# A row of token scales for two feed-forwards: matmuls with ones against a trip through DRAM

## The chip, the cores and the metric

One core of a Trainium2 chip runs one launch of the kernel. The metric is the device time of that launch in microseconds (us), the median of several runs.

## What is computed

The layer works on 256 tokens of 1024 channels, in fp32. It has a feed-forward, a mixer of three branches (retention, differential attention, attention into 256 memory tokens) and a second feed-forward. Only the feed-forwards matter here:

```
x = x + 0.5 * (silu(h @ wg) * (h @ wu)) @ wd      with  h = rms_norm(x) * gain
```

with `wg` and `wu` of 1024 x 2816 and `wd` of 2816 x 1024. The norm is one number r per token, 1/sqrt(mean(x^2) + eps). Since r is constant along the channels, the kernel multiplies `x * gain` by the weights first and applies r to the product.

## The kernel before, in words

**Products in three parts.** Every weight tile is split into a rounded part `hi` (ScalarE, L131) and a rest `lo` (VectorE, L134, in two halves); activations are split in the same way. A product is the sum of three matmuls. The results of gate and up lie with hidden channels on partitions and the 256 tokens along the free axis, so r is needed there as a row of 256 numbers that is the same on all 128 partitions.

**The feed-forward (`ffn`, L296).** The hidden width is cut into 11 blocks of 256. `gate_up(j)` multiplies block j of gate and up (weights loaded on SyncE's queue at L123; matmuls at L167 with `hi`, at L172 with `lo`) and joins the parts on ScalarE (L182) and VectorE (L183) into a tile `jo`. `hidden` turns the two `jo` of a block into the operand of the down product: L303 multiplies gate's tile by the row `rb` on VectorE, L304 takes Silu on ScalarE, L305 multiplies by up's tile on VectorE, L308 (ScalarE) and L309 (VectorE) split the product into `ah` and `al`. The down matmuls (L191, L192, L194) accumulate into `acc`. Blocks 0 and 1 of gate and up run ahead of the row, and then block 2 runs on TensorE before the down product of block 0.

**The row (`token_rstd`, L483, and `rows_to_free`, L234).** ScalarE sums the squares of x (L488), VectorE makes the mean (L231), GpSimd raises it to -0.5 (L226): r, two numbers on each of 128 partitions. L238 multiplies the identity by r's two columns, two diagonal tiles `dg`; L239 multiplies a matrix of ones by them in fp32 on TensorE, which spreads the row to all partitions in a PSUM bank; L241 copies it to `rb`. L492 makes r/2 for the residual.

**What sets the order.** A planner sorts the instructions of each engine by its own estimate of when their operands are ready, and by the order in which the program names them; each engine then runs its list strictly in that order. `keep(...)` pins an instruction behind the one that the program named last on the same engine. `tc.issue_after(i)` puts what its block names on the engine of i behind i: block 2's VectorE work stands behind `st["dg"]` (L323), which is the second diagonal tile. Tiles of `mid` (`jo`, `dg`, `rb`, `ah`, `al` among them) share 14 slots, and the two PSUM tags `pj` and `at` have four banks each.

**GpSimd's queue around the change.** GpSimd runs r (L226) and then, pinned behind it, the load of the columns of gains `vcol` (L363, called by the hook of block 1). These gains are first used by ScalarE at L245 on the memory tokens.

The lines that the steps touch most:

```python
def rows_to_free(r, alloc):
    dg = mid([NT, P], F32, "dg")
    ps = alloc([S])
    for t in range(NT):
        st["dg"] = V.tensor_scalar_mul(dg[:, t, :], ident, r[:, t:t + 1]).ins
        keep(T.matmul(ps[:, t * P:(t + 1) * P], ones, dg[:, t, :], start=True, stop=True))
    rb = mid([S], F32, "rb")
    V.tensor_copy(rb, ps)
    return rb
```

Of the kernel before, what the change touches and what calls it, by code (L numbers as in the profile page):

```python
# [11 lines left out]
F32 = mybir.dt.float32  # L12
# [7 lines left out]
P = 128  # L20
D = 1024
S = 256
NT = S // P
# [33 lines left out]
def layer_kernel(ctx, tc, a):  # L57
    nc = tc.nc
    V, A, G, T = nc.vector, nc.scalar, nc.gpsimd, nc.tensor
    keep = tc.keep_in_program_order  # L60
# [3 lines left out]
    wp = ctx.enter_context(tc.tile_pool(name="wp", bufs=3))  # L64
    tp = ctx.enter_context(tc.tile_pool(name="tp", bufs=14))
    sp = ctx.enter_context(tc.tile_pool(name="sp", bufs=24))
    pp = ctx.enter_context(tc.tile_pool(name="pp", bufs=4, space=PSUM))

    cnt = [0]

    def nm(s):
        cnt[0] += 1
        return f"{s}_{cnt[0]}"

    def big(shape, dt=F32, n="g"):
        return gp.tile([P] + shape, dt, tag="g", name=nm(n))

    def mid(shape, dt=F32, n="t"):
        return tp.tile([P] + shape, dt, tag="t", name=nm(n))

    def small(n, nme="s"):
        return sp.tile([P, n], F32, tag="s", name=nm(nme))

    def const(shape, n, dt=F32):
        return cp.tile([P] + shape, dt, tag=n, name=n)

    def psj(shape):
        return pp.tile([P] + shape, F32, tag="pj", name=nm("pj"))

    def psa(shape):  # L90
        return pp.tile([P] + shape, F32, tag="at", name=nm("at"))
# [22 lines left out]
    def wchunk(w, k0, kt, n0, n, deint=False, parts=1):  # L114
        shape = [kt, n]
        raw = wp.tile([P] + shape, F32, tag="raw", name=nm("raw"))
        hi = wp.tile([P] + shape, F32R, tag="hi", name=nm("hi"))
        lo = wp.tile([P] + shape, F32R, tag="lo", name=nm("lo"))
        src = w[k0 * P:(k0 + kt) * P, n0:n0 + n].rearrange("(k p) n -> p k n", p=P)
        step = kt // parts  # L120
        for q in range(parts):
            c = slice(q * step, (q + 1) * step)
            nc.sync.dma_start(raw[:, c, :], src[:, c, :])  # L123
        for q in range(parts):
            c = slice(q * step, (q + 1) * step)
            rv, hv, lv = raw[:, c, :], hi[:, c, :], lo[:, c, :]
            hb = hv.bitcast(F32)
            if deint:
                rv = rv.rearrange("p k (i e) -> p k e i", e=2)
                hv, lv, hb = (v.rearrange("p k (e i) -> p k e i", e=2) for v in (hv, lv, hb))  # L130
            A.copy(hv, rv)  # L131
            h = step // 2
            for e in (slice(0, h), slice(h, step)):
                V.tensor_sub(lv[:, e], rv[:, e], hb[:, e])  # L134
        return hi, lo
# [50 lines left out]
    def mm_b(ps, w, xT, t, k0, kt, first, last, c0=0, n=512):  # L186
        hi, lo = w
        tk = slice(t * P, (t + 1) * P)
        c = slice(c0, c0 + n)
        for k in range(kt):  # L190
            T.matmul(ps, xT.h(k0 + k)[:, tk], hi[:, k, c], start=(first and k == 0), stop=False)  # L191
            T.matmul(ps, xT.l(k0 + k)[:, tk], hi[:, k, c], start=False, stop=False)  # L192
        for k in range(kt):
            T.matmul(ps, xT.h(k0 + k)[:, tk], lo[:, k, c], start=False, stop=(last and k == kt - 1))  # L194
# [19 lines left out]
    def proj_s(w, n0, xT, deint=False, alloc=None):  # L214
        ps = [(alloc or psj)([2, S]) for _ in range(2)]
        wc = wchunk(w, 0, KT, n0, 256, deint)
        mm_s(ps, wc, xT, turns=alloc is not None)
        return joined(ps)


    st = {}
# [9 lines left out]
        V.tensor_scalar(ms, ss, 1.0 / count, EPS, ALU.mult, ALU.add)  # L231
        return pow_rstd(ms, n, out)

    def rows_to_free(r, alloc):  # L234
        dg = mid([NT, P], F32, "dg")
        ps = alloc([S])
        for t in range(NT):
            st["dg"] = V.tensor_scalar_mul(dg[:, t, :], ident, r[:, t:t + 1]).ins  # L238
            keep(T.matmul(ps[:, t * P:(t + 1) * P], ones, dg[:, t, :], start=True, stop=True))  # L239
        rb = mid([S], F32, "rb")  # L240
        V.tensor_copy(rb, ps)  # L241
        return rb

    def split_gain(src, col, hi, lo):
# [5 lines left out]
    vcol = const([NCOL], "vcol")  # L250
# [3 lines left out]
    def col(i):  # L254
        return vcol[:, i:i + 1]

    ident = const([P], "ident")
    ones = const([P], "ones")
# [37 lines left out]
    def ffn(xT, w, rb, hooks, first, alloc, end=None):  # L296
        wg, wu, wd = w
        acc = []
        state = {}

        def hidden(sg, av):
            rv = state["rb"].unsqueeze(1).broadcast_to([P, 2, S])
            V.tensor_mul(sg, sg, rv)  # L303
            A.activation(sg, sg, AF.Silu)  # L304
            V.tensor_mul(av, av, sg)  # L305
            ah = mid([2, S], F32R, "ah")
            al = mid([2, S], F32R, "al")
            A.copy(ah, av)  # L308
            V.tensor_sub(al, av, ah.bitcast(F32))  # L309
            return Hidden(ah, al)  # L310

        def gate_up(j, alloc=None):
            return proj_s(wg, j * 256, xT, alloc=alloc), proj_s(wu, j * 256, xT, alloc=alloc)

        raw = [first, gate_up(1, alloc)]
        state["rb"] = rb()
        ready = [hidden(*p) for p in raw]
        for j in range(NPAIR):
            aT = ready.pop(0)
            if j in hooks:  # L320
                hooks[j]()
            if j == 0:
                with tc.issue_after(st["dg"]):  # L323
                    ready.append(hidden(*gate_up(j + 2)))
            elif j + 2 < NPAIR:
                ready.append(hidden(*gate_up(j + 2)))
            wc = wchunk(wd, 2 * j, 2, 0, D)
            if j == 0:
                acc = [[psa([512]) for _ in range(2)] for _ in range(NT)]
            if end and j == NPAIR - 2:  # L330
                held = wc, aT
                continue
            if end and j == NPAIR - 1:
                for t, c0, n in end:
                    ps = acc[t][c0 // 512][:, 0:n] if c0 % 512 == 0 else psj([n])
                    fresh = c0 % 512 != 0
                    mm_b(ps, *held, t, 0, 2, fresh, False, c0, n)
                    mm_b(ps, wc, aT, t, 0, 2, False, True, c0, n)
                acc.append(ps)
                continue  # L340
            for t in range(NT):
                for hf in range(2):
                    mm_b(acc[t][hf], wc, aT, t, 0, 2, j == 0, j == NPAIR - 1, hf * 512)
        return acc
# [6 lines left out]
    rows = const([288], "rows")  # L351
# [8 lines left out]
    lamr = rows[:, 32:288].rearrange("p (i d) -> p i d", d=DDK)  # L360

    def vcols():
        keep(G.dma_start(vcol, a["cols"]))  # L363
        keep(V.tensor_scalar_mul(col(G_SUB), col(G_SUB), 1.0 - LAM_INIT))
        keep(V.memset(vcol[0:ROT, G_DQ:G_DQ + 2], 1.0))
        keep(V.memset(vcol[64:64 + ROT, G_DQ:G_DQ + 2], 1.0))
        keep(V.tensor_mul(gqk, vcol[:, G_MQ:G_MQ + 2], vcol[:, G_MK:G_MK + 2]))
# [109 lines left out]
    def stats1():  # L477
        xv = a["x"].rearrange("(t p) d -> p t d", p=P)
        for t in range(NT):
            nc.sync.dma_start(x[:, t, :], xv[:, t, :])  # L480
        return token_rstd(psa, "half1")

    def token_rstd(alloc, name, behind=None):  # L483
        ss = small(NT, "ss")
        j = big([NT, D], F32, "sq")
        with tc.issue_after(behind) if behind else nullcontext():
            for t in range(NT):
                A.activation(j[:, t, :], x[:, t, :], AF.Square, accum_out=ss[:, t:t + 1])  # L488
        r = rstd_of(ss, NT, D)
        rb = rows_to_free(r, alloc)  # L490
        st[name] = const([NT], name)
        V.tensor_scalar_mul(st[name], r, 0.5)  # L492
        return rb

    def mem_load():
# [19 lines left out]
    w1s = (a["ffn1_w_gate"], a["ffn1_w_up"], a["ffn1_w_down"])  # L515
    pgu = first_ffn1()
    acc = ffn(st["xT"], w1s, stats1, hooks, pgu, psj)


# [54 lines left out]
    for b in range(2):  # L574
        ps = proj_b(w_kv, b * 512, memT)
        for t in range(NT):
# [3 lines left out]
            r = rstd_of(ss, 2, MDH)  # L580
# [8 lines left out]
    for b in range(2):  # L589
        ps = proj_b(w_kv, D + b * 512, memT)  # L590
# [58 lines left out]
    for b in range(2):  # L649
        ps = proj_b(w_in, O_MQ + b * 512, hT)  # L650
# [66 lines left out]
    for b in range(2):  # L717
        ps = proj_b(w_in, O_DV + b * 512, hT)
# [213 lines left out]
    for n in range(2):  # L932
        ps = [psj([512]) for _ in range(NT)]
# [9 lines left out]
    acc = [[psa([512]) for _ in range(2)] for _ in range(NT)]  # L943
    xT = Pair("fp")
# [38 lines left out]
    pgu = first_ffn2()  # L983
    gfin = big([D], F32, "gfin")
    G.dma_start(gfin, a["final_norm"].partition_broadcast(P))
    w2s = (a["ffn2_w_gate"], a["ffn2_w_up"], a["ffn2_w_down"])
    end = ((0, 0, 512), (0, 512, 512), (1, 0, 512), (1, 512, 256), (1, 768, 256))
    acc = ffn(xT, w2s, lambda: token_rstd(psj, "half2", st["fp"]), {}, pgu, psa, end)
    ov = a["out"].rearrange("(t p) d -> p t d", p=P)
    o = big([NT, D], F32, "o")  # L990

# [119 lines left out]
```

## Time and profile before

| | before |
|---|---|
| runs, median (lowest to highest of 3) | 878.5 us (878.47 to 878.6) |
| the profiled execution | 878.89 us, of which 877.1 us are the span |
| granted TensorE clock, mean | 0.999 of full speed |
| TensorE matmul busy | 869.6 us, 99% of the span |
| VectorE busy | 603.4 us, 69% |
| ScalarE busy | 444.6 us, 51% |
| GpSimd busy | 41.4 us, 5% |
| moved by DMA | 162.25 MB, 185 GB/s in the mean |

The span is the stretch from the first to the last instruction of the profiled execution; the rest of its time lies around it. PE is TensorE's matmul, PEld its weight load, DVE VectorE, ACT ScalarE, POOL GpSimd, SP SyncE's queue.

### The profile page before, as it was taken

The page shows a single profiled execution, that of the slowest core. Times are in us where ns is not written, and L with a number is a line of the kernel's source. Part 1 is how long each engine was busy: PE and PEld are TensorE (multiplying, and loading weights), DVE is VectorE, ACT ScalarE, POOL GpSimd, SP SyncE. Part 2 cuts the span into 40 slices and gives each one's busy share as a digit, 9 for nine tenths or more (in the row PEclk, how much of TensorE's full clock was granted, in tenths as well). Part 3 has the DMA queues.
Part 4 walks back from the last instruction along what each step waited for, and adds up shares of the span by engine and source line. Part 5 has one row for each costly group of instructions (what it writes and reads, how often), then busy time and mean ns, then how long its engine had stood idle before and what let it go on. Part 6 is the DMA issues. An engine that isn't in the chain of part 4 may idle for free.

```text
span 877.1 us, 11343 instructions
## 1 busy us (share of the span) xinstructions
PE 869.6 (99%) x4436; PEld 738.0 (84%) x4436; DVE 603.4 (69%) x979; ACT 444.6 (51%) x595; POOL 41.4 (5%) x47
## 2 busy tenths in 40 slices
PE   9999999999999999999999999999999999999997
PEld 7888888888888888878888888888888888888885
DVE  6889856667676866669696677665566676666664
ACT  6854644456544445645554444444433665444442
POOL 0010000001032010000100000000000000000000
PEclk9999999999999999999999999999999999999999
DMA  9975555555554554345454555545555466565531
GB/s 340 333 253 192 193 191 190 194 182 175 174 189 166 194 179 159 121 147 174 145 200 151 171 192 192 202 169 190 189 175 197 135 211 218 176 202 189 177 124 49
DMA packets 100693, 162.25 MB, mean 185 GB/s; under 512 B 2896, under 2 KB 55904, under 8 KB 100640
## 3 DMA queue, kind: packets, MB, share of 16 engines
q1 hardware_dynamic: 99648, 159.00, 53.2%
q0 software_dynamic: 848, 2.40, 1.0%
q8 instruction: 35, 0.57, 0.2%
q10 hardware_dynamic: 144, 0.13, 0.0%
q14 instruction: 18, 0.15, 0.0%
HBM read 160.47 MB, written 1.05 MB: 184 GB/s over the span
## 4 chain that ended last, share of the span: by engine, by line
PE 99%; DVE 0%; ACT 0%; POOL 0%; issue 0%; POOLq 0%
PE pj L167 20%; PE pj L191 14%; PE pj L192 14%; PE pj L194 14%; PE pj L172 10%; PE at L192 5%; PE at L191 5%; PE at L194 5%; PE at L261 2%; PE at L201 2%; PE at L460 1%; PE at L167 1%; PE at L735 1%; PE at L463 0%; PE at L276 0%; PE at L172 0%
## 5 line engine op out<-in xcount | busy, mean ns | idle before, releaser
L134 DVE TENSOR_TENSOR lo<-raw,hi 128x1024 fp32r<-128x1024 f32 (+1 forms) x292 | 347.1, 1205 | 173.5 <-ACT hi L131 173.2
L131 ACT CAST hi<-raw 128x2048 fp32r<-128x2048 f32 (+1 forms) x146 | 276.4, 1895 | 259.7 <-issue 132.1
L191 PE MATMUL pj<-hi,hp 128*128 128x512 f32 x352 | 139.3, 396 | 0.0
L192 PE MATMUL pj<-hi,hp 128*128 128x512 f32 x352 | 137.3, 390 | 0.0
L194 PE MATMUL pj<-lo,hp 128*128 128x512 f32 x352 | 94.2, 389 | 0.0
L191 PEld LDWEIGHTS pj<-hi,hp 128*128 128x128 f32 x352 | 66.2, 188 | 13.9 <-issue 1.0
L194 PEld LDWEIGHTS pj<-lo,hp 128*128 128x128 f32 x352 | 66.1, 188 | 13.9
L167 PE MATMUL pj<-fp,hi 128*128 128x512 f32 x320 | 77.5, 391 | 0.0
L192 PEld LDWEIGHTS pj<-hi,hp 128*128 128x128 f32 x352 | 66.2, 188 | 13.0
L167 PE MATMUL pj<-xp,hi 128*128 128x512 f32 x320 | 76.6, 390 | 0.0
L167 PEld LDWEIGHTS pj<-xp,hi 128*128 128x128 f32 x320 | 59.2, 188 | 11.7
L167 PEld LDWEIGHTS pj<-fp,hi 128*128 128x128 f32 x320 | 59.0, 188 | 11.9 <-DVE fp L246 0.4
L192 PE MATMUL at<-hi,al 128*128 128x512 f32 (+1 forms) x176 | 68.2, 388 | 0.0
L191 PE MATMUL at<-hi,ah 128*128 128x512 f32 (+1 forms) x176 | 68.1, 387 | 0.0
L226 POOL TENSOR_TENSOR rstd<-ms,expo 128x2 f32<-128x2 f32 (+3 forms) x26 | 30.0, 1155 | 699.4 <-DVE ms L231 525.5
L194 PE MATMUL at<-lo,ah 128*128 128x512 f32 (+1 forms) x176 | 53.8, 387 | 0.0
L172 PEld LDWEIGHTS pj<-fp,lo 128*128 128x128 f32 x320 | 41.8, 191 | 2.1
L172 PEld LDWEIGHTS pj<-xp,lo 128*128 128x128 f32 x320 | 41.3, 191 | 1.7
L172 PE MATMUL pj<-fp,lo 128*128 128x256 f32 x320 | 42.4, 282 | 0.0
L172 PE MATMUL pj<-xp,lo 128*128 128x256 f32 x320 | 41.8, 283 | 0.0
L194 PEld LDWEIGHTS at<-lo,ah 128*128 128x128 f32 x176 | 32.9, 188 | 6.8
L183 DVE TENSOR_TENSOR jo<-pj,jo 128x256 f32<-128x256 f32 x96 | 36.3, 415 | 3.1 <-ACT jo L182 3.1
(279 smaller groups left out, 1211.2 us busy)
## 6 DMA issues: line engine op xcount, KB each, us to landing
raw<-in_w_in SPq DMA_DIRECT2D x52, 1024.0 KB, 4.8
raw<-in_ffn_w_down SPq DMA_DIRECT2D x22, 1024.0 KB, 4.7
raw<-in_ffn_w_gate SPq DMA_DIRECT2D x20, 1024.0 KB, 5.1
raw<-in_ffn_w_up SPq DMA_DIRECT2D x20, 1024.0 KB, 5.1
raw<-in_mem_w_kv SPq DMA_DIRECT2D x8, 1024.0 KB, 4.9
raw<-in_ret_w_o SPq DMA_DIRECT2D x8, 1024.0 KB, 4.8
raw<-in_mem_w_o SPq DMA_DIRECT2D x4, 1024.0 KB, 4.8
raw<-in_diff_w_o SPq DMA_DIRECT2D x4, 1024.0 KB, 4.7
```

The costliest lines, as they stand in the source:

```text
L131: A.copy(hv, rv)
L134: V.tensor_sub(lv[:, e], rv[:, e], hb[:, e])
L167: T.matmul(ps[nt], hi[:, k, nt * P:(nt + 1) * P], xT.both(k), start=(first and k == k0), stop=False, skip_group_check=True)
L172: T.matmul(ps[nt][:, 0, :], lo[:, k, nt * P:(nt + 1) * P], xT.h(k), start=False, stop=(last and k == k1 - 1), skip_group_check=True)
L183: V.tensor_add(o[:, nt, :], ps[nt][:, 0, :], o[:, nt, :])
L191: T.matmul(ps, xT.h(k0 + k)[:, tk], hi[:, k, c], start=(first and k == 0), stop=False)
L192: T.matmul(ps, xT.l(k0 + k)[:, tk], hi[:, k, c], start=False, stop=False)
L194: T.matmul(ps, xT.h(k0 + k)[:, tk], lo[:, k, c], start=False, stop=(last and k == kt - 1))
L201: T.matmul(o, l, r, start=(i == 0), stop=(i == n - 1))
L226: G.tensor_tensor(r, ms, expo[:, :n], ALU.pow)
L261: T.transpose(out, in_, ident)
L460: T.matmul(ps[nt], hi[:, nt * P:(nt + 1) * P], xT.both(k), start=(k == 0), stop=False, skip_group_check=True)
```

## The change

The diagonal tiles, the fp32 matmuls, the PSUM bank and the copy go. GpSimd's queue stores r (two numbers of each partition) as a row of 256 in a DRAM tile and loads that row back to all 128 partitions. Between the two, the first feed-forward issues the load of `vcol`, which the hook of block 1 no longer issues. `st["dg"]` is now L492's product, so block 2's VectorE work stands behind that.

```diff
+    dp = ctx.enter_context(tc.tile_pool(name="dp", bufs=2, space=bass.MemoryType.DRAM))
...
-    def rows_to_free(r, alloc):
-        dg = mid([NT, P], F32, "dg")
-        ps = alloc([S])
-        for t in range(NT):
-            st["dg"] = V.tensor_scalar_mul(dg[:, t, :], ident, r[:, t:t + 1]).ins
-            keep(T.matmul(ps[:, t * P:(t + 1) * P], ones, dg[:, t, :], start=True, stop=True))
+    def rows_to_free(r, between=None):
+        d = dp.tile([S], F32, tag="rows", name=nm("rows"))
+        keep(G.dma_start(d.rearrange("(t p) -> p t", p=P), r))
+        if between:
+            between()
         rb = mid([S], F32, "rb")
-        V.tensor_copy(rb, ps)
+        keep(G.dma_start(rb, d.partition_broadcast(P)))
         return rb
...
     def vcols():
-        keep(G.dma_start(vcol, a["cols"]))
...
-        return token_rstd(psa, "half1")
-
-    def token_rstd(alloc, name, behind=None):
+        return token_rstd("half1", between=lambda: keep(G.dma_start(vcol, a["cols"])))
+
+    def token_rstd(name, behind=None, between=None):
...
-        rb = rows_to_free(r, alloc)
+        rb = rows_to_free(r, between)
         st[name] = const([NT], name)
-        V.tensor_scalar_mul(st[name], r, 0.5)
+        st["dg"] = V.tensor_scalar_mul(st[name], r, 0.5).ins
...
-    acc = ffn(xT, w2s, lambda: token_rstd(psj, "half2", st["fp"]), {}, pgu, psa, end)
+    acc = ffn(xT, w2s, lambda: token_rstd("half2", st["fp"]), {}, pgu, psa, end)
```

## Rows read from the trace of the kernel before

**Rows 1.** The page: busy time, share of the span and instructions of each engine.

```profile
span 877.1 us, 11343 instructions
PE 869.6 (99%) x4436; PEld 738.0 (84%) x4436; DVE 603.4 (69%) x979; ACT 444.6 (51%) x595; POOL 41.4 (5%) x47
```

**Rows 2.** Waits of PE, whole span: all there are (us in total, times, longest).

```profile
PE at L276 <- DVE expo L273: 1.1, 1, 1.1
```

**Rows 3.** Timeline, first feed-forward, PE (start us, us, engine, line, operation).

```profile
24.96 1.12 PE L172 MATMUL pj<-xp,lo 128*128 128x256 f32 x8
...
25.91 2.00 PE L167 MATMUL pj<-xp,hi 128*128 128x512 f32 x8
...
27.75 1.11 PE L172 MATMUL pj<-xp,lo 128*128 128x256 f32 x8
...
28.70 0.60 PE L239 MATMUL at<-dg,ones 128*128 128x128 f32 x4
...
29.06 3.92 PE L167 MATMUL pj<-xp,hi 128*128 128x512 f32 x16
```

**Rows 4.** Timeline, second feed-forward, PE.

```profile
708.94 1.11 PE L172 MATMUL at<-fp,lo 128*128 128x256 f32 x8
...
709.89 0.60 PE L239 MATMUL pj<-dg,ones 128*128 128x128 f32 x4
...
710.25 3.92 PE L167 MATMUL pj<-fp,hi 128*128 128x512 f32 x16
```

**Rows 5.** Timeline of POOL around the first row.

```profile
23.66 0.72 POOL L226 TENSOR_TENSOR rstd<-ms,expo 128x2 f32<-128x2 f32 x1 [22.35 <-DVE ms L231]
24.33 0.72 POOL L363 DMA_DIRECT2D vcol<-in_cols  x1
43.26 0.54 POOL L403 DMA_DIRECT2D pi<-in_positions  x1 [18.21 <-DVE al L309]
```

**Rows 6.** DMA issues: tile, queue, count, KB each, median us from issue to landing.

```profile
memT<-in_memT SPq DMA_DIRECT2D x1, 1024.0 KB, 9.1
...
out<-o SPq DMA_DIRECT2D x3, 256.0 KB, 2.0
...
rows<-in_rows POOLq DMA_DIRECT2D x1, 144.0 KB, 7.2
pi<-in_positions POOLq DMA_DIRECT2D x1, 128.0 KB, 3.9
...
vcol<-in_cols POOLq DMA_DIRECT2D x1, 15.5 KB, 5.1
...
pci<-in_positions POOLq DMA_DIRECT2D x1, 1.0 KB, 6.9
```

**Rows 7.** Timeline, first feed-forward, DVE from the third `jo` to the first `al`.

```profile
28.78 0.42 DVE L183 TENSOR_TENSOR jo<-pj,jo 128x256 f32<-128x256 f32 x1 [1.91 <-ACT jo L182]
29.12 3.49 DVE L134 TENSOR_TENSOR lo<-raw,hi 128x1024 fp32r<-128x1024 f32 x3
...
32.86 0.41 DVE L241 COPY rb<-at 128x256 f32<-128x256 f32 x1
33.19 1.21 DVE L134 TENSOR_TENSOR lo<-raw,hi 128x1024 fp32r<-128x1024 f32 x1
34.32 1.28 DVE L303 TENSOR_TENSOR jo<-jo,rb 128x512 f32<-128x512 f32 x2
...
39.00 0.68 DVE L309 TENSOR_TENSOR al<-jo,ah 128x512 fp32r<-128x512 f32 x1
```

**Rows 8.** Timeline, first feed-forward: ACT's first use of `vcol`, PE after the row.

```profile
31.80 2.91 ACT L245 ACTIVATE xp<-memT,vcol 128x256 fp32r<-128x256 f32 x7 [0.32 <-DMA memT<-in_memT]
...
32.82 2.08 PE L172 MATMUL pj<-xp,lo 128*128 128x256 f32 x16
...
40.30 0.19 PEld L192 LDWEIGHTS at<-hi,al 128*128 128x128 f32 x1
```

**Rows 9.** Busy us by engine (instructions) in stretches, granted clock, DMA share, GB/s.

```profile
25.00:30.00 5.00, 5.00 (x33) 4.54 (x32) 2.04 (x5) 3.90 (x5) 0.05 (x1) 1.00 1.05 399
30.00:35.00 5.00, 5.00 (x32) 4.42 (x31) 5.00 (x8) 4.39 (x9) 0.00 (x0) 1.00 0.89 319
...
40.00:45.00 5.00, 5.00 (x25) 4.20 (x25) 5.00 (x10) 3.76 (x7) 1.74 (x4) 1.00 0.71 227
```

**Rows 10.** Timeline, second feed-forward: the row's source, DVE's use of it, PE's need.

```profile
697.73 0.17 DVE L492 TENSOR_SCALAR half<-rstd 128x2 f32<-128x2 f32 x1 [0.84 <-POOL rstd L226]
...
713.24 1.28 DVE L303 TENSOR_TENSOR jo<-jo,rb 128x512 f32<-128x512 f32 x2
...
721.49 0.19 PEld L192 LDWEIGHTS at<-hi,al 128*128 128x128 f32 x1
```

## The prediction

> **What bounds the kernel now.** I read the page's first part, then the waits of TensorE, then the timeline around the two places where the row is made. TensorE's matmuls are busy for 869.6 of 877.1 us [rows 1], and the only wait of TensorE that the trace has is 1.1 us at the start [rows 2]. From there to the end TensorE goes from one matmul to the next, so it is the bound in both feed-forwards: what TensorE no longer does comes off the time in full, what the other engines no longer do comes off nothing, and what they do later costs nothing until TensorE waits for it. Two questions are left: how much TensorE time the fp32 matmuls take, and whether the row still comes before its use.
>
> **What is removed from TensorE.** In the first feed-forward the matmuls with ones start at 28.70 and the next product at 29.06 [rows 3]. I take starts, not the busy time of 0.60 us in the same row, since matmuls overlap. The group before them starts at 27.75, which is 0.95 us ahead; an undisturbed change from such a group to the next product is 24.96 to 25.91, also 0.95 us [rows 3]. So the change-over itself costs nothing extra, and the four passes (two matmuls, which the trace shows as x4) hold TensorE for 29.06 - 28.70 = 0.36 us. The second feed-forward has the same: 0.95 from 708.94 to 709.89, then 0.36 to 710.25 [rows 4]. The sum is 2 x 0.36 = 0.72 us. If the busy time were the true cost, it would be 2 x 0.60 = 1.20 us; I keep that as the other end.
>
> **What is removed elsewhere.** VectorE loses two diagonal tiles and one copy of 0.41 us (L241) per feed-forward. VectorE is not the bound [rows 1, 2], so this gains nothing directly; it matters once below, where VectorE's list is tight. The freed PSUM bank and the freed slot of the 14 gain nothing either, as TensorE waits for neither [rows 2].
>
> **What is added: a store and a load, one after the other.** Before, the row's path is r, diagonal, matmul, copy, and ends at 33.27 (32.86 + 0.41) in the first feed-forward [rows 7], though r is there at 24.4 (23.66 + 0.72) [rows 5]: the matmuls are pinned behind block 1's. After, GpSimd issues the store at about 24.4, in the place where it now issues `vcol` (24.33). The load waits for the store to land.
>
> The trace has no store on GpSimd's queue. From below I bound it by the stores of the output on SyncE's queue, 2.0 us; from above by `pci`, a load of the same 256 single numbers in the same arrangement, 6.9 us, which stood behind four other transfers of its queue [rows 6]. I take 5.1 us, that of `vcol`: small, 128 partitions, the same queue, issued at the same moment with the DMA engines just as full (share 1.05 in 25 to 30 us) [rows 6, 9]. For the load the nearest row is `pi`, which is the same shape, 256 numbers spread to 128 partitions, first in its queue: 3.9 us. It ran at a DMA share of 0.71, and mine runs at 0.89 [rows 9], so the upper end is `rows`, 7.2 us; I take 3.9 and keep the upper end [rows 6]. The row then lands at 24.4 + 5.1 + 3.9 = 33.4 us, between 24.4 + 2.0 + 3.9 = 30.3 and 24.4 + 6.9 + 7.2 = 38.5.
>
> [...]
>
> **When the row is needed.** From the start of L303 at 34.32 to the end of the first `al` at 39.68 VectorE has 5.36 us of its list, without a gap [rows 7]. TensorE loads `al` as weights at 40.30 [rows 8]; with 0.36 us gone it asks at 39.94. So L303 may start as late as 39.94 - 5.36 = 34.58 us. The landing at 33.4 leaves 1.2 us. VectorE itself comes to L303 at about 34.0, since the copy (33.19 - 32.86 = 0.33 us of its list) is gone. No wait, at my values; at the upper end 38.5 - 34.58 = 3.9 us of waiting on TensorE.
>
> In the second feed-forward r is there at 697.7, L303 ran at 713.24 and TensorE loads `al` at 721.49 [rows 10]. Even the slow ends, 6.9 + 7.2 us, bring the row at 711.8. This place costs nothing.
>
> **What is moved.** `vcol` is issued behind the store, about 0.7 us later (the store's own issue, priced by `vcol`'s 0.72 [rows 5]), and lands near 24.4 + 0.7 + 5.1 = 30.2. Its first user waits until 31.80, for `memT` [rows 8], issued earlier with 9.1 us to landing [rows 6]: covered by 1.6 us. Without that cover ScalarE's eight small pieces, and the Silu behind them, would shift. Behind the load, which now blocks GpSimd's queue until the store lands, stands `pi` at 43.26 [rows 5], 10 us later. The extra 129 KB per feed-forward are 0.3 us of DMA time at the 399 GB/s of 25 to 30 us [rows 9]; the weights that this delays are behind ScalarE's split, and TensorE shows no wait for them [rows 2]. Block 2's VectorE work may now stand up to two diagonal tiles earlier in the list, which can only help TensorE. All of these I cost at nothing.
>
> **Sum.** The profiled execution took 878.89 us, 0.39 above the median of the runs; 878.89 - 0.72 = 878.17, and against the median of 878.5 this is 877.8 us. A measurement of this kernel can tell about 0.2% from no change, 1.76 us; the gain is 0.08%.
>
> **Rivals.**
>
> *The row holds VectorE (slower).* VectorE runs its list in order, and the planner places L303 by its own estimate of the two transfers, which I cannot see. If it believes that the row comes early, it may place the first L303 behind the `jo` of 28.78 and ahead of the three splits of 29.12 [rows 7], the first two of which make the `lo` that TensorE takes at 32.82 [rows 8], or 32.46 after the change. Then a row at 33.4 gives the two halves at 33.4 + 0.64 + 2 x 1.16 = 36.4 (0.64 is half of L303's 1.28, 1.16 a third of 3.49), while TensorE comes to the second half four matmuls after 32.46, at about 33.0 (4 x 2.08/16): a wait of 3.4 us, and 878.5 - 0.72 + 3.4 = 881.2. With the list as before, a landing at 38.5 gives 878.5 - 0.72 + 3.9 = 881.7. It decides as slower once TensorE waits over 2.5 us. For it: nothing in the trace says that the planner's estimate is near 5 us; DMA is full here. Against it: VectorE was already late in these splits, and the landing has 1.2 us to spare with the old list. [...] Chance 0.22.
>
> *The gain is given back (no change).* The row lands somewhat late, between 34.6 and 37 us, and TensorE waits 0.1 to 2.4 us: 877.9 to 880.2 us. Chance 0.20.
>
> *More than the matmuls (faster).* A shorter list on VectorE and a freed PSUM bank let TensorE run closer. It needs over 1.76 us, and TensorE has no wait to give back [rows 2]; even the busy time of the removed matmuls is 1.20. Chance 0.05.
>
> **How the numbers follow.** My forecast, no wait and 0.72 us gained, has 0.53. No change by 0.2% is the forecast and the gain given back: 0.73; slower 0.22; faster 0.05. The likeliest time is 877.8. The low end is 878.5 - 1.20 = 877.3, with 0.2 for the spread of the runs 877.1; the high end takes in the gain given back (880.2) and the smaller waits of the slower rival: 880.8. Outside lie the faster case and the larger half of the slower one.
>
> **What would show it.** In the profile after, L239 and L241 are gone and the matmul groups around their places start 0.95 us apart, which is the 0.36 gained twice. The store should land near 29.5 and the load near 33.4; `pi` stays behind both. TensorE's waits show no line in the first 60 us beyond the 1.1 us at the start. I am wrong if TensorE waits for VectorE's `lo` or `al` near 32 to 40 us, with VectorE idle ahead of L303 until the load lands; or if the time falls by more than 1.2 us, which would mean that TensorE lost time that its waits do not show.

## The result and the profile after

The kernel after took 889.76 us (median of 4 runs, 888.88 to 890.95) against 878.55 us before (4 runs, 878.47 to 878.63): a ratio of 1.0128 with a 95% interval of 1.0115 to 1.014. It is slower, by far more than the 0.2% that a measurement can tell. The profiled execution took 890.95 us, with a span of 889.2 us against 877.1 [rows 1]. Line numbers around the change move up by one: L134 is L135, L167 is L168, L172 is L173, L183 is L184. L303 stays where it was; the store is L237, the load L241. In the fences below, `...` stands for lines that are left out.

The page of the kernel after (span, busy time of each engine):

```profile
span 889.2 us, 11332 instructions
PE 871.4 (98%) x4428; PEld 739.1 (83%) x4428; DVE 602.1 (68%) x973; ACT 444.0 (50%) x595; POOL 44.0 (5%) x51
```

The removed matmuls are gone (8 fewer), yet TensorE is busy 1.8 us longer, and the span has grown by 12.1 us. The waits of TensorE, all there are (us in total, times, longest):

```profile
PE pj L168 <- DVE jo L184: 10.3, 1, 10.3
PE at L276 <- DVE expo L273: 1.1, 1, 1.1
```

The second line was there before [rows 2]; the first is new, a single wait of 10.3 us for a `jo`. Its place is seen in the timeline of VectorE and TensorE around the first row (start us, us, engine, line, operation, count, idle before and its releaser):

```profile
29.38 1.22 DVE L135 TENSOR_TENSOR lo<-raw,hi 128x1024 fp32r<-128x1024 f32 x1
...
34.01 2.00 PE L168 MATMUL pj<-xp,hi 128*128 128x512 f32 x8
...
43.52 1.29 DVE L303 TENSOR_TENSOR jo<-jo,rb 128x512 f32<-128x512 f32 x2 [12.93 <-DMA rb<-rows]
...
45.87 0.41 DVE L184 TENSOR_TENSOR jo<-pj,jo 128x256 f32<-128x256 f32 x1
...
46.34 3.78 PE L168 MATMUL pj<-xp,hi 128*128 128x512 f32 x8 [10.32 <-DVE jo L184]
...
49.92 3.01 PE L173 MATMUL pj<-xp,lo 128*128 128x256 f32 x16
```

VectorE ends a split at 30.6 and stands still for 12.93 us at L303, until the row lands. Behind L303 on its list stands the `jo` (L184) that empties a PSUM bank, the last `jo` of block 1, and TensorE, which has run out of banks at 36.0, gets that bank at 46.3. In the kernel before, this `jo` stood ahead of L303 (timeline of VectorE, where L303 starts at 34.32):

```profile
32.52 0.42 DVE L183 TENSOR_TENSOR jo<-pj,jo 128x256 f32<-128x256 f32 x1
```

Then a second loss is seen: the eight matmuls behind the wait take 3.78 us where eight such took 2.00 at 34.01, and the sixteen of L173 take 3.01 where sixteen took 2.08 before [rows 8].

Why the row is late stands in GpSimd's timeline and in the DMA issues of 24 to 46 us (KB each, median us from issue to landing):

```profile
24.43 0.89 POOL L237 DMA_DIRECT2D rows<-rstd  x1 [0.30 <-POOL rstd L227]
25.32 0.58 POOL L480 DMA_DIRECT2D vcol<-in_cols  x1
36.38 0.54 POOL L241 DMA_DIRECT2D rb<-rows  x1 [10.48 <-DMA rows<-rstd]
```

```profile
raw<-in_ffn_w_gate SPq DMA_DIRECT2D x1, 1024.0 KB, 14.1
raw<-in_ffn_w_up SPq DMA_DIRECT2D x1, 1024.0 KB, 14.4
rb<-rows POOLq DMA_DIRECT2D x1, 128.0 KB, 7.0
rows<-rstd POOLq DMA_DIRECT2D x1, 1.0 KB, 11.7
vcol<-in_cols POOLq DMA_DIRECT2D x1, 15.5 KB, 11.0
```

The store of 1 KB takes 11.7 us, the load 7.0: 24.4 + 11.7 + 0.3 + 7.0 = 43.4. Transfers that are under way beside the store are late too: `vcol` took 5.1 us before [rows 6] and takes 11.0. The stretches say the same (columns as in [rows 9]):

```profile
25.00:30.00 5.00, 5.00 (x30) 4.41 (x30) 4.79 (x6) 4.17 (x5) 0.90 (x2) 1.00 1.29 386
30.00:35.00 5.00, 5.00 (x31) 4.44 (x31) 0.59 (x1) 0.59 (x2) 0.00 (x0) 1.00 0.79 42
35.00:40.00 5.00, 1.02 (x5) 0.51 (x3) 0.00 (x0) 0.00 (x0) 0.54 (x1) 0.84 0.67 146
40.00:45.00 5.00, 0.00 (x0) 0.00 (x0) 1.48 (x3) 0.75 (x2) 0.00 (x0) 0.50 0.70 249
45.00:50.00 5.00, 3.66 (x9) 2.92 (x10) 4.95 (x11) 3.56 (x5) 0.00 (x0) 0.50 0.14 19
50.00:55.00 5.00, 5.00 (x27) 4.62 (x26) 5.00 (x8) 4.11 (x8) 2.82 (x5) 0.80 0.94 363
```

In 30 to 35 us the DMA engines are shown as busy (0.79) while they move 42 GB/s; before, a share of 0.89 moved 319 [rows 9]. The granted clock falls to 0.50 (40 to 50 us) after TensorE stood still from 36.0 on, and has a mean of 0.80 still in 50 to 55 us.

The span closes on this: 10.3 of wait, plus 2.7 for the matmuls at the low clock (3.78 - 2.00 + 3.01 - 2.08), minus the 0.72 gained, is 12.3; the span grew by 12.1.

In the second feed-forward TensorE's matmuls wait for nothing, though VectorE waits 5.80 us for the row. Timeline of VectorE and TensorE, and the two transfers among the DMA issues of 706 to 730 us:

```profile
726.78 1.29 DVE L303 TENSOR_TENSOR jo<-jo,rb 128x512 f32<-128x512 f32 x2 [5.80 <-DMA rb<-rows]
...
732.93 0.68 DVE L309 TENSOR_TENSOR al<-jo,ah 128x512 fp32r<-128x512 f32 x1
...
733.67 0.49 PE L193 MATMUL at<-hi,al 128*128 128x512 f32 x1
```

```profile
rb<-rows POOLq DMA_DIRECT2D x1, 128.0 KB, 6.8
rows<-rstd POOLq DMA_DIRECT2D x1, 1.0 KB, 8.9
```

This is only just in time: the first `al` ends at 733.61, TensorE's load of it as weights waited 0.2 us, and the matmul with it starts at 733.67.

### The profile page after: what moved, and what is told of

The parts are those of the page before. It is cut to its first block, busy times and chain, and to the rows that moved or that the text cites. A ratio compares the mean times of both kernels' runs of the same rounds, so it can differ in the third digit from the quotient of the medians.

```text
span 889.2 us, 11332 instructions
## 1 busy us (share of the span) xinstructions
PE 871.4 (98%) x4428; PEld 739.1 (83%) x4428; DVE 602.1 (68%) x973; ACT 444.0 (50%) x595; POOL 44.0 (5%) x51
## 3 DMA queue, kind: packets, MB, share of 16 engines
HBM read 160.74 MB, written 1.05 MB: 182 GB/s over the span
## 4 chain that ended last, share of the span: by engine, by line
PE 93%; DMA 4%; DVE 1%; issue 1%; ACT 0%; SPq 0%; POOL 0%; POOLq 0%; ACTq 0%; DVEq 0%
PE pj L168 19%; PE pj L192 14%; PE pj L193 14%; PE pj L195 14%; PE pj L173 10%; PE at L193 5%; PE at L192 5%; PE at L195 5%; PE at L261 2%; PE at L202 2%; DMA raw<-in_ffn_w_up 2%; DMA rows<-rstd 1%; PE at L168 1%; DMA rb<-rows 1%; PE at L734 1%
## 5 line engine op out<-in xcount | busy, mean ns | idle before, releaser
L135 DVE TENSOR_TENSOR lo<-raw,hi 128x1024 fp32r<-128x1024 f32 (+1 forms) x292 | 347.1, 1205 | 175.2 <-ACT hi L132 174.9
L168 PE MATMUL pj<-xp,hi 128*128 128x512 f32 x320 | 78.5, 397 | 10.3 <-DVE jo L184 10.3
L168 PEld LDWEIGHTS pj<-xp,hi 128*128 128x128 f32 x320 | 60.2, 192 | 22.7 <-DVE jo L184 10.7
L168 PE MATMUL pj<-fp,hi 128*128 128x512 f32 x320 | 77.4, 391 | 0.0
L168 PEld LDWEIGHTS pj<-fp,hi 128*128 128x128 f32 x320 | 59.0, 188 | 11.8 <-DVE fp L246 0.4
L173 PEld LDWEIGHTS pj<-xp,lo 128*128 128x128 f32 x320 | 42.4, 196 | 1.8
L173 PEld LDWEIGHTS pj<-fp,lo 128*128 128x128 f32 x320 | 41.8, 191 | 2.1
L173 PE MATMUL pj<-xp,lo 128*128 128x256 f32 x320 | 42.8, 287 | 0.0
L173 PE MATMUL pj<-fp,lo 128*128 128x256 f32 x320 | 42.4, 282 | 0.0
L193 PEld LDWEIGHTS at<-hi,al 128*128 128x128 f32 x176 | 33.1, 188 | 6.3 <-DVE al L309 0.2
```

Of the source, the lines that this page charges most:

```text
L168: T.matmul(ps[nt], hi[:, k, nt * P:(nt + 1) * P], xT.both(k), start=(first and k == k0), stop=False, skip_group_check=True)
L173: T.matmul(ps[nt][:, 0, :], lo[:, k, nt * P:(nt + 1) * P], xT.h(k), start=False, stop=(last and k == k1 - 1), skip_group_check=True)
```

## Experiments

The theory: the store is slow because of what it writes, it is slow beside full DMA engines (11.7 us, with a DMA share of 1.29 from 25 to 30 us) and also beside nearly idle ones (8.9 us; the second store was issued at 710.4, and from 710 to 715 us the DMA share was 0.01), and through VectorE's list it stops TensorE. The rivals: GpSimd's queue is what is slow; any small transfer is slow there; the order of VectorE's list is the fault, not the row; the low clock is the larger part.

### Where the loss is: the first feed-forward by matmuls again (second_only)

```diff
-        rb = rows_to_free(r, between)
+        rb = rows_by_matmul(r, alloc) if alloc else rows_to_free(r, between)
...
```

`rows_by_matmul` is the function of the kernel before, and the load of `vcol` goes back to block 1's hook.

> The first feed-forward makes its row by matmuls again, the second by the trip through DRAM. Theory (the whole loss is TensorE's wait of 10.3 us and the lower clock after it in the first feed-forward; the second only loses its matmuls, 0.36 us): 878.55 - 0.36 = 878.2 us, no wait of TensorE after the start, and VectorE again idle ahead of L303 for about 5.8 us in the second. Rival (the slow store and the late weights in the second feed-forward cost time too): above 879.

Measured: 878.05 us against 878.78 (ratio 0.9993, 0.9984 to 1.0002). So the loss is in the first feed-forward. The second keeps its slow store and loses nothing that can be measured, since there TensorE has work that needs no row: VectorE waits 5.0 us for the row, and TensorE, whose matmuls have no wait but the one at the start, multiplies with the first `al` from 720.97. The two transfers among the DMA issues of its second feed-forward:

```profile
rb<-rows POOLq DMA_DIRECT2D x1, 128.0 KB, 6.2
rows<-rstd POOLq DMA_DIRECT2D x1, 1.0 KB, 9.0
```

### The load without the store (load_only)

```diff
-        d = dp.tile([S], F32, tag="rows", name=nm("rows"))
-        keep(G.dma_start(d.rearrange("(t p) -> p t", p=P), r))
+        d = a["b_gate"][0:S]
```

> No store: the row is loaded to all partitions from 256 numbers of an input (b_gate), so the scales in both feed-forwards are other numbers. Theory A (the store is what makes the row late, and the DMA engines slow for all): the load is issued near 24.4 us and lands in 4 to 5 us, as pi did; weights and memT land as in the kernel before; TensorE does not wait and the time is 878.6 - 0.7 = 877.9 us, the forecast's own sum. Rival (the load alone is slow, 7.0 us, and enough to stop TensorE through VectorE's list): the load lands at 7 us and the time stays above 879.

This kernel multiplies by other numbers, so it does not compute the layer; it shows the time alone. Measured: 877.91 us against 878.61 (0.9991, 0.9981 to 1.0). The load took 5.4 us, over the 4 to 5 expected. No wait of TensorE but the one at the start. VectorE's list has the order of the kernel after, L303 ahead of the `jo`, and it costs nothing here, because the row is there in time (timeline of VectorE):

```profile
30.51 1.29 DVE L302 TENSOR_TENSOR jo<-jo,rb 128x512 f32<-128x512 f32 x2
```

So the list by itself makes no loss; it takes a late row. And this is the most that the change could give: the 0.7 us of the removed matmuls.

### The store without the load (store_beside)

The kernel before, with a store more in `token_rstd` and the DRAM pool for it; nobody reads what it stores.

```diff
...
+        d = dp.tile([S], F32, tag="rows", name=nm("rows"))
+        keep(G.dma_start(d.rearrange("(t p) -> p t", p=P), r))
```

> The kernel before, with both stores added and read by nobody; the row is made by matmuls. Theory A, with the pieces holding the DMA engines for every queue: memT, vcol and the weights issued from 22 to 31 us land in 11 to 14 us instead of 5 to 9, and the megabyte of w_down next to the second store in about 10; the time rises by 0 to 3 us, since the weights have some us to spare. Rival (the late weights after the change come only from slots that VectorE frees late): landing times as before, time 878.6.

Measured: 883.17 us, 1.0048 (1.0034 to 1.0062): 4.4 us lost by stores that nothing waits for, more than the 0 to 3 expected. DMA issues of 20 to 46 us:

```profile
memT<-in_memT SPq DMA_DIRECT2D x1, 1024.0 KB, 14.6
...
raw<-in_ffn_w_gate SPq DMA_DIRECT2D x1, 1024.0 KB, 11.3
raw<-in_ffn_w_up SPq DMA_DIRECT2D x1, 1024.0 KB, 11.5
rows<-rstd POOLq DMA_DIRECT2D x1, 1.0 KB, 12.1
```

`memT` takes 14.6 us where it took 9.1 [rows 6], though it is on another queue, and `vcol` takes 11.4 where it took 5.1. ScalarE has its use of these two ahead of Silu: after 6.54 us of idle time it starts on them at 36.91, and on Silu at 39.72 (timeline of ScalarE):

```profile
36.91 2.91 ACT L246 ACTIVATE xp<-memT,vcol 128x256 fp32r<-128x256 f32 x7 [6.54 <-DMA memT<-in_memT]
...
39.72 1.13 ACT L305 ACTIVATE jo<-jo 128x512 f32<-128x512 f32 x2
```

TensorE then waits 1.7 us for `ah` and 1.1 for `al`. The store thus slows transfers on SyncE's queue as well as on its own.

### What makes the store slow (sync_store, packed_store, spread_store, one_row_store, spread_64)

First the queue:

```diff
-        keep(G.dma_start(d.rearrange("(t p) -> p t", p=P), r))
+        keep(nc.sync.dma_start(d.rearrange("(t p) -> p t", p=P), r))
```

> The store is issued on SyncE's queue, the load stays on GpSimd's; same 256 pieces of 4 bytes. Theory A (the pieces are the price, on whichever queue): the store still takes about 10 us, TensorE waits about 9 us, time 888 to 890. Theory C (GpSimd's queue is the price): the store lands in 2 to 3 us like the stores of the output, the row is there near 34 us, TensorE does not wait and the time is 877.8 to 879.

Measured: 887.84 us (1.0102, 1.0086 to 1.0117). The stores take 8.8 and 8.7 us, a little under the 10 expected, and TensorE still waits 6.9 us. The queue is at most a part of the price: 2.9 of the 11.7 us in the first feed-forward, 0.2 of the 8.9 in the second.

Then pieces of 8 bytes in place of 4, the two numbers of a partition side by side (L303 reads the row with a stride, in four halves):

```diff
-        keep(G.dma_start(d.rearrange("(t p) -> p t", p=P), r))
+        keep(G.dma_start(d.rearrange("(p t) -> p t", t=NT), r))
...
```

> The row lies in DRAM as partition-major pairs: the store writes 128 pieces of 8 bytes instead of 256 of 4, and L303 reads the row with a stride of two (four products in place of two, on halves). Theory A (the number of small pieces written to DRAM is the price): the stores land in about half their time, near 6 us in the first feed-forward (11.7 after the change) and 4.5 in the second (8.9); L303 starts near 38 us instead of 43.5, TensorE waits about 5 us instead of 10.3, time about 883. Theory B (the store stands behind the weights' megabytes on full DMA engines): stores still at 11.7 and 8.9 us, time about 890.

Measured: 884.83 us (1.007, 1.0056 to 1.0084). The stores fall to 7.3 and 3.2 us, and the wait for the `jo` to 5.7. So the arrangement of the pieces matters, but this changes their size, their number and their distance at once.

So the distance alone, in the arrangement of store_beside, where nothing reads the row: each word in a block of 512 bytes of its own, and then 64 bytes apart (`[S, 16]`); and one piece of 1 KB from one partition (a row of `x`, other numbers). The first edit, against store_beside:

```diff
-        d = dp.tile([S], F32, tag="rows", name=nm("rows"))
-        keep(G.dma_start(d.rearrange("(t p) -> p t", p=P), r))
+        d = dp.tile([S, P], F32, tag="rows", name=nm("rows"))
+        keep(G.dma_start(d.rearrange("(t p) c -> p t c", p=P)[:, :, 0], r))
```

> As store_beside (the kernel before, with stores of r that nobody reads), but each of the 256 words goes to a block of 512 bytes of its own in DRAM. Theory D (the words are slow because they fall into the same blocks of DRAM, from all 16 engines at once): the stores land in 2 to 4 us instead of 12.1 and 9.1, memT lands near 9 us, and the time is that of the kernel before. Theory E (each small piece costs by itself, wherever it lies): landing times and time as in store_beside, 883.

> As store_beside, but the same 1 KB is stored from one partition, as one contiguous row of x (other numbers, read by nobody). If the pieces are the price, the store lands in 2 to 3 us, memT and the weights land as in the kernel before and the time is 878.6. If any store on this queue is slow next to full DMA engines, it lands in over 6 us in the first feed-forward.

> As spread_store, but the 256 words stand 64 bytes apart instead of 512. If words 64 bytes apart no longer hinder each other, the stores land as in spread_store (4.9 and 2.2 us) and the time is 878.6. If eight neighbours in 512 bytes still do, they land between that and store_beside's 12.1 and 9.1 us, and memT lands later than 9 us.

| stored beside the kernel before | store, first / second feed-forward | ratio |
|---|---|---|
| 256 words side by side (store_beside) | 12.1 / 9.1 us | 1.0048 (1.0034 to 1.0062) |
| 256 words, 64 bytes apart (spread_64) | 4.9 / 2.3 us | 1.0 (0.9991 to 1.0009) |
| 256 words, 512 bytes apart (spread_store) | 4.9 / 2.2 us | 1.0001 (0.9992 to 1.001) |
| one piece of 1 KB (one_row_store) | 5.1 / 1.9 us | 1.0004 (0.9994 to 1.0013) |

The same 256 words, from the same 128 partitions, on the same queue: 64 bytes between them take away 7.2 and 6.8 us, and the loss of time with it. In the first feed-forward the three fast stores took more than the 2 to 4 us expected, and in the second about that. The issues of 20 to 46 us with words 64 bytes apart, against those of store_beside above:

```profile
memT<-in_memT SPq DMA_DIRECT2D x1, 1024.0 KB, 8.5
...
rows<-rstd POOLq DMA_DIRECT2D x1, 1.0 KB, 4.9
vcol<-in_cols POOLq DMA_DIRECT2D x1, 15.5 KB, 5.0
```

So the number of pieces is not the price, nor that a piece is a single word, nor how many partitions they come from: it is that the words are neighbours in DRAM (12.1 us against 4.9). Between 4 and 64 bytes no distance was tried. What the memory or the DMA engine does with neighbours, no run shows; the words 64 bytes apart, eight of which lie in each 512 bytes, took no longer than those 512 bytes apart (4.9 and 2.3 us against 4.9 and 2.2).

### A trip with few pieces (few_pieces)

VectorE transposes r in blocks of 32 x 32, so that each of four partitions holds 32 numbers in a row; two stores of four pieces of 128 bytes.

```diff
...
-        keep(G.dma_start(d.rearrange("(t p) -> p t", p=P), r))
+        rt = const([32], "rt" + nm("r"))
+        V.transpose(rt, rs)
+        for t in range(NT):
+            keep(G.dma_start(d[t * P:(t + 1) * P].rearrange("(b q) -> b q", q=32), rt[t:P:32, :]))
...
```

> The change with 8 pieces in place of 256: r is written into a tile of 32 columns, VectorE transposes its blocks of 32x32, and two stores of four rows of 128 bytes each make the row in DRAM; the load is as in the change. Theory (the number of pieces is the price): the stores land in 2 to 3.5 us, the row is there at 31 to 33 us, TensorE waits for less than 1 us, and the time is 877.9 to 878.9 us: at or a little below the kernel before. Rival (a trip through DRAM is slow in itself): stores over 6 us, time over 881.

Measured: 881.22 us (1.0034, 1.0023 to 1.0046), over the expected 877.9 to 878.9. The stores took 4.8 us, more than the 2 to 3.5 expected and far less than 11.7. With the transpose, two issues and a load of 4.9 us the row comes at 36.2, not at 31 to 33, and the `jo` behind L303 still holds TensorE. Waits of TensorE, and L303 in VectorE's timeline:

```profile
PE pj L168 <- DVE jo L184: 2.4, 1, 2.4
```

```profile
36.21 1.29 DVE L309 TENSOR_TENSOR jo<-jo,rb 128x512 f32<-128x512 f32 x2 [5.26 <-DMA rb<-rows]
```

Behind this short wait the eight matmuls took 2.11 us and the sixteen after them 2.08; the granted clock of this execution was 0.999 in the mean.

### The order of VectorE's list (pinned, packed_pinned, few_pinned)

The work of blocks 0 and 1 on the row is put behind the last `jo` of block 1, so that the row can't hold that bank:

```diff
-            V.tensor_add(o[:, nt, :], ps[nt][:, 0, :], o[:, nt, :])
+            st["jo"] = V.tensor_add(o[:, nt, :], ps[nt][:, 0, :], o[:, nt, :]).ins
...
-        ready = [hidden(*p) for p in raw]
+        with tc.issue_after(st["jo"]):
+            ready = [hidden(*p) for p in raw]
```

> The change, with L303 of blocks 0 and 1 put behind block 1's last jo (L184) in VectorE's list. Theory (TensorE stops early because that jo, which frees its PSUM bank, stands behind L303): TensorE finishes block 2 near 40 us, waits there for ah and al until about 48.8, and the time falls by about 4 us, to 886. Rival (the order does not matter, since the row's time sets the end): 889.8.

Measured: 891.54 us (1.0143, 1.0126 to 1.016), where the theory wanted 886. The wait for the `jo` is gone, and another stands in its place (waits of TensorE):

```profile
PE at L192 <- ACT ah L308: 8.7, 1, 8.7
PE at L193 <- DVE al L309: 1.1, 2, 0.7
```

TensorE goes a little further and then lacks the operand that the row makes (0.4 us of the second line is in the second feed-forward). From the start of L303 to block 3's first product it took 58.39 - 44.39 = 14.0 us, against 58.23 - 43.52 = 14.7 after: the pin is worth 0.7 us, and the row came 0.9 later. The pin moves the wait; it doesn't remove it, and the rival of this expectation, that the row's time sets the end, was nearer.

> Both: 128 pieces of 8 bytes, and L303 behind block 1's last jo. If the two causes add up, packed_store's 884.8 falls by its wait of 5.7 us less what is left until al: the row lands at 38.7, al near 43, TensorE asks at 39.9: a wait of about 3 us, 878.6 - 0.7 + 3 = 881. If the order does nothing, 884.8.

Pin and 8-byte pieces: 885.48 us (1.0074, 1.0059 to 1.0089), where 881 was expected; the row came at 39.8 and TensorE waited 4.0 us for `ah`.

> few_pieces with one store of eight pieces instead of two stores, and L303 of blocks 0 and 1 behind block 1's last jo. Theory (the end is the row's time plus the list from L303 to the first al, once no bank of PSUM stands behind the row): the row is there near 35 us, TensorE waits 0 to 1.5 us for al, time 878.0 to 879.5. Rival (al is held by block 3's lo, which now stands ahead of it in VectorE's list, and whose weights come late): a wait of over 2 us, time over 880.

Pin and a single store of eight pieces of 128 bytes: 879.52 us (1.0014, 1.0005 to 1.0023), at the upper end of the 878.0 to 879.5 expected, its 11 runs from 878.27 to 882.26. The profiled execution took 878.27, the shortest of them, and its matmuls have no wait but the one at the start; the first load of `al` as weights waited 0.4 us for VectorE. L303 in VectorE's timeline, and the two transfers among the DMA issues of 20 to 46 us:

```profile
34.54 1.29 DVE L308 TENSOR_TENSOR jo<-jo,rb 128x512 f32<-128x512 f32 x2 [2.40 <-DMA rb<-rows]
```

```profile
rb<-rows POOLq DMA_DIRECT2D x1, 128.0 KB, 4.5
...
rows<-rtr POOLq DMA_DIRECT2D x1, 1.0 KB, 4.8
```

With transfers of about the length that the prediction took (4.8 and 4.5 us against 5.1 and 3.9), the kernel stands at the edge: L303 starts at 34.54, and the prediction had 34.58 as the last start without a wait. That other runs, whose traces were not taken, lie over the edge would explain their spread, but that is argued, not shown.

### What the clock costs (fill)

Fifty matmuls of ones (100 passes) keep TensorE busy ahead of the matmul that waits.

```diff
...
+            if fill and f is upper and nt == 0:
+                wt = psa([P])
+                for _ in range(FILL):
+                    keep(T.matmul(wt, ones, ones, start=True, stop=True))
...
```

> The change, with 50 matmuls of ones (results unused) put ahead of the matmul that waits in the first feed-forward, so that TensorE works through most of its wait. Theory (about 2.6 us of the loss is the lower granted clock after the idle stretch): the granted clock stays at 1.00 from 35 to 55 us, the eight matmuls after the wait take 2.0 us instead of 3.8 and the next sixteen 2.1 instead of 3.0, time about 887. Rival (these matmuls are slow for another reason): 889.8.

Measured: 890.0 us (1.0129, 1.0113 to 1.0144), not the 887 expected. The clock did stay up (timeline of TensorE, and a stretch with the granted clock):

```profile
36.00 11.33 PE L183 MATMUL at<-ones 128*128 128x128 f32 x100
...
47.46 2.08 PE L169 MATMUL pj<-xp,hi 128*128 128x512 f32 x8
...
49.38 2.08 PE L174 MATMUL pj<-xp,lo 128*128 128x256 f32 x16
```

```profile
45.00:50.00 5.00, 4.87 (x35) 4.37 (x35) 5.00 (x8) 3.20 (x4) 0.00 (x0) 1.00 0.00 2
```

From L303 to block 3's first product it took 56.76 - 44.64 = 12.1 us, against 58.23 - 43.52 = 14.7 after: 2.6 us less, which is the 2.7 of the closure and a fifth of the 12.1 us. But in the profiled execution the store took 12.5 us and the row came 1.1 us later; and in the second feed-forward, where the store took 10.1 us, TensorE now waited for `al` (timeline of TensorE):

```profile
733.19 0.50 PE L198 MATMUL at<-hi,al 128*128 128x512 f32 x1 [0.83 <-DVE al L314]
```

The span of after with these three, 889.2 + 1.1 - 2.6 + 0.8 = 888.5, is close to the 888.7 of this kernel. So in this execution the clock's part is borne out, and the later rows of both feed-forwards hide it.

### All of them by the time of the row

Start of L303 and span are those of the profiled execution, in us; the median is that of all runs.

| kernel | first L303 starts | span | median |
|---|---|---|---|
| load_only | 30.51 | 876.2 | 877.91 |
| before | 34.32 | 877.1 | 878.55 |
| few_pinned | 34.54 | 876.5 | 879.52 |
| few_pieces | 36.21 | 879.1 | 881.22 |
| packed_store | 38.76 | 883.5 | 884.83 |
| packed_pinned | 39.78 | 883.9 | 885.48 |
| sync_store | 40.20 | 886.2 | 887.84 |
| after | 43.52 | 889.2 | 889.76 |
| pinned | 44.39 | 889.9 | 891.54 |
| fill | 44.64 | 888.7 | 890.0 |

Before 34.6 us a row that is earlier gives nothing more; behind it the span grows by more than the row is late (from few_pieces to after 10.1 us for 7.3), part of it the clock. Fill, whose clock stayed up through a long wait, lies below the others. No version beats the kernel before clearly: second_only is the lowest of those that compute the layer, and its interval takes in 1.

## Why the prediction was wrong

It said 877.8 us, between 877.1 and 880.8, with no wait. Step by step:

- **The removed matmuls: right.** In the second feed-forward after, the lines around the lost place start at 721.35 and 722.31, 0.96 us apart; 0.36 gained. In the first they start 0.95 apart. load_only, with nothing but this left, took 877.91 us.
- **The store, taken as 5.1 us and at most 6.9: the step that failed.** It took 11.7 us. Of the 10.0 us by which the row came later than the 33.4 that was forecast (43.4), 6.6 are the store's, 3.1 the load's and 0.3 the load's issue. The value was taken from `vcol`, which fits a store of spread words (4.9) or of one piece (5.1) at the same moment. The upper end was taken from `pci`, a load of single words into 128 partitions; no row of before had single words written side by side in DRAM.
- **What the store does to others, costed at 0.3 us of DMA time: wrong by the same cause.** The load took 7.0 us where 3.9 was taken and 7.2 was the upper end. In load_only, with no store ahead, from another source and at an earlier moment, it took 5.4; whether the other 1.6 come from the held-up weights that move in the kernel after was not tried. `vcol` landed at 36.3 instead of 30.2, and `memT` took 5 us longer. After, these are hidden, as ScalarE stands anyway until L303 is done; store_beside shows what they cost when they are not.
- **The last start of L303, 34.58: near for the old order of `jo` and L303** (few_pinned started it at 34.54, with the weight load of `al` 0.4 us late), **and 1.4 us too late for the new one.** In the kernel after the `jo` stands behind L303, and from L303's start to the release of TensorE it is 46.34 - 43.52 = 2.82 us, so L303 had to start by 36.0 - 2.8 = 33.2. The prediction's own formula with the true row gives 43.52 - 34.58 = 8.9 us of wait, the trace 10.3.
- **The slower rival had the right mechanism** (the row holds VectorE's list, and TensorE waits for what stands behind it) and the wrong place: it looked at the `lo` of the splits and at `al`, not at the `jo` that frees a bank. Its condition, a wait of over 2.5 us, was met four times over. Its prices, 881.2 and 881.7, came from the same too small store.
- **The clock was not in it.** That TensorE comes back from a wait of 10.3 us at 0.50 and loses 2.7 us more had no row in the trace of before, where TensorE waits only 1.1 us, at the start.
- **The second feed-forward: right in the outcome only.** The upper ends were 6.9 + 7.2 and a row at 711.8; it took 8.9 + 6.8. The margin that the prediction counted on was used up: `al` was ready 0.06 us before TensorE used it, in fill, whose row came later still, TensorE waited 0.8 us there, and in pinned 0.4.

With the true row the prediction's own steps give 878.5 - 0.72 + 8.9 = 886.7 us, and the clock's 2.7, for which it had no term, brings 889.4, against 889.76 measured. So the late row is most of the miss. That the sum comes so close is in part luck: the wait in the trace is 10.3 and not 8.9, in an execution of 890.95 us.

## What to carry to other kernels

Price a DMA by its pieces and where they land, not by its bytes (1 KB took 12.1 us as neighbouring words and 4.9 as words 64 bytes apart): a column of one word per partition that is written out as a dense row is a bad store here, and a 32 x 32 transpose ahead of it, which makes a few pieces of 128 bytes, takes it from 11.7 to 4.8 us. Even so, the trip was not faster here than the matmuls (879.5 to 881.2 us against 878.6 to 878.7). When a value starts to come by a trip through DRAM, walk down the list of each engine that waits for it and look for what frees a PSUM bank or makes an operand; a slack of 1.2 us is no slack when one term has no row to price it. And if the bound engine hardly waits in the trace, ask what a wait would cost beyond its length (here 2.7 us on 10.3).

## What the runs showed of the hardware

- Words of 4 bytes written side by side into 1 KB of DRAM from 128 partitions took 8.7 (sync_store) to 12.5 us (fill) in every profiled execution with such a store; the same words 64 bytes apart (spread_64) took 4.9 us where the DMA share was 1.05 (25 to 30 us), and 2.3 in the second feed-forward, where the DMA engines were busy for less than a tenth of the time.
- Such a store slowed transfers on SyncE's queue: `memT` went from 9.1 to 14.6 us in store_beside, and in the kernel after 42 GB/s were moved at a DMA share of 0.79 (30 to 35 us).
- After waits of TensorE of 10.3 us (after), 6.9 (sync_store) and 5.7 (packed_store) the granted clock was 0.50 (45 to 50 us in after, 40 to 45 in the other two), and the eight matmuls behind the wait took 3.78 us in after and sync_store instead of 2.00; after a wait of 2.4 us (few_pieces) they took 2.11.
